# Two zero-padded copies of the rotary key: 128-row score products for the B heads

## The chip, the core and the metric

The kernel runs on one core of one Trainium2 chip. The metric is the device time of one execution in microseconds (us). The core has TensorE (PE, matrix products, with a queue of weight loads shown as PEld), VectorE (DVE), ScalarE (ACT), GpSimd (POOL) and SyncE (SP, which here only starts DMA transfers). Matrix products read SBUF and write PSUM.

## The reference

One residual block of a streaming encoder for 256 tokens of width 2048: a gated feed-forward layer, a mixer with two attention branches A and B, a cross attention to 256 memory tokens, and a second feed-forward layer, each followed by a layer norm. The change touches branch B, cut here to what matters:

```python
q = (c_q @ w_q_b).reshape(b, s, B_HEADS, QK_NOPE + QK_ROPE)        # 16 heads, 128 + 64
q_nope, q_pe = jnp.split(q, [QK_NOPE], axis=-1)
q = jnp.concatenate([q_nope, apply_rope(q_pe, cos, sin)], axis=-1)
k_pe = apply_rope(k_pe[:, :, None, :], cos, sin)                   # one rotary key for all heads
k = jnp.concatenate([k_nope, jnp.broadcast_to(k_pe, ...)], axis=-1)
sc = jnp.einsum('bqhd,bkhd->bhqk', qb, k) * scale                  # masked by chunks, softmax, times v
```

Every head's score is a product over 128 features without position plus one over 64 rotary features. The rotary key is the same for all 16 heads.

## The kernel before, in words

Activations are kept turned, features on the 128 partitions and tokens along the row, so that they can be operands of PE. Weights come in units of 1 MB by SP's queue, and each unit is split by ACT ("hi", a cast to a rounded format) and DVE ("lo", the remainder, L245) so that PE can multiply it in two or three passes with near-fp32 accuracy. Two such units are held at a time. A list of work items (`add`, L143; `run`, L168) is issued in order, and a scheduler then orders each engine's instructions by priorities.

The stages around the change, all in `mixer` (from L783):

- `lat_scale` and `lat_turn` (L850, L868) normalise the low-rank inputs of B and transpose them on PE (L876); ACT (L880) and DVE (L881) empty the PSUM tiles.
- `kpe` (L892) computes the rotary key. A wide product leaves two halves in a PSUM tile, `total` (L269) adds them (L273 on ACT, L274 on DVE) into a work tile `a`. The weight columns were doubled on the host, so rows 0 to 63 and rows 64 to 127 of `a` hold the same 64 features. `swap` (L887) copies blocks of 32 rows crosswise from `a` to `b` with four transfers on SP's queue (L890). DVE then forms a*cos (L897), b*sin (L898) and their sum (L899) in `krope`, 128 rows by 256 tokens.
- `gb_apply` (L434) is woven into this time: gains and biases come by POOL's queue (L440, L441) and DVE applies them (L444, L445).
- The 8 pairs of A heads follow, then the 16 B heads. The rotary queries `rt` hold two heads per tile: an even head in rows 0 to 63, the odd one in rows 64 to 127.
- Per B head h, in this order: `b_scores(h)`, `b_trans(h-1)`, `b_proj(h+2)`, `b_out(h-1)`. `b_scores` calls `scores` (L916), which issues four fp32 products, each of which becomes two instructions on PE (L921): for the first 128 queries against 128 keys and for the second 128 queries against 256 keys, first the part without position (128 rows), then the rotary part (64 rows, upper or lower half by the head's parity). DVE scales and masks (L1037), and `softmax` runs on DVE and ACT (L761 to L768). `b_trans` transposes the probabilities on PE (L773) and ACT copies them (L779). `b_proj` makes queries and keys of head h+2 (L255 on PE, L1026 on ACT and DVE) and, for every fourth head, the values of four heads (L286, L1011). `b_out` multiplies values and probabilities (L962, L963) and splits the result (L234, L235).
- The output projections follow (L299), and later `mem_norm` (L1141) normalises the memory tokens; its `spread` (L1170) multiplies a matrix of ones by diagonal matrices on PE.

A matrix `ones` of 128x128 is kept for the whole kernel: the first use is a run of 12 products at the start (L474), the last is `spread`. Small per-row values (`sm`) have four buffers per name.

Of the kernel before, what the change touches and what calls it, by code (L numbers as in the profile page):

```python
# [9 lines left out]
F32 = mybir.dt.float32  # L10
F32R = mybir.dt.float32r
I32 = mybir.dt.int32
AF = mybir.ActivationFunctionType
ALU = mybir.AluOpType
# [3 lines left out]
P = 128  # L18
S = 256
# [72 lines left out]
class Kernel:  # L92
# [34 lines left out]
    def w1(self, shape=(P, S), dt=F32):  # L127
        return self.work.tile(list(shape), dt, tag="w1", bufs=6, name=self.name("w1"))

    def sm(self, tag, n, dt=F32):  # L130
        return self.small.tile([P, n], dt, tag=tag, name=self.name(tag))

    def mm_tile(self):
        return self.ps_mm.tile([P, 512], F32, tag="mm", name=self.name("mm"))
# [243 lines left out]

    def ln_scale(self, st):
        nc = self.nc  # L380
        mv, v, y, a = self.sm("mv", 2), self.sm("v", 1), self.sm("y", 1), self.sm("a", 1)
        nc.vector.bn_aggr(mv, st)
        nc.vector.tensor_scalar(v, mv[:, 1:2], LN_EPS, None, ALU.add)
        self.rsqrt(v, y, a)
        nb = self.sm("nb", 1)
        self.chain = nc.vector.scalar_tensor_tensor(nb, mv[:, 0:1], -1.0, y, ALU.mult, ALU.mult)
        return mv[:, 0:1], y, nb

# [58 lines left out]

    def setup(self):
        nc, t = self.nc, self.t
        self.ones = self.const.tile([P, P], F32, name="ones")  # L450
        nc.vector.memset(self.ones, 1.0)
        nc.scalar.activation(self.sm("first", 1), self.ones[:, 0:1], AF.Silu)
        self.vecs = self.const.tile([P, N_VEC], F32, name="vecs")
        self.rope = self.const.tile([P, 2, S], F32, name="rope")
        self.ident = self.const.tile([P, P], F32, name="ident")
        make_identity(nc, self.ident)
        self.mask = self.const.tile([P, 3 * P], F32, name="mask")
        nc.gpsimd.memset(self.mask, 0.0)
        self.mask_out(self.mask)
        self.krope = self.const.tile([P, S], F32, name="krope")  # L460
        self.h = [self.res.tile([P, D], F32, tag=f"h{i}", name=f"h{i}") for i in range(2)]

    def mask_out(self, b):
# [319 lines left out]
    def mixer(self, xT, st, steps):  # L783
        nc, t = self.nc, self.t
        SPANS = ((0, P), (P, 3 * P))
        e = self.__dict__
# [4 lines left out]
        def val(n, tts, g, ps, tags=None, held=0, keep=False, again=False):  # L791
            def fn(w=None):
                if keep:
                    kept[g] = w
                w = kept.pop(g) if again else w
                for tt in tts:
                    if g == 0:
                        ps[tt] = self.mm_tile()
                    self.mm_tok(ps[tt], tt, w, xT(), range(4 * g, 4 * g + 4), g == 0, g == 3)
                if g == 3:  # L800
                    if "t" not in va:
                        va["t"] = self.block("H4", (P, 2, 1024))
                    for tt in tts:
                        (nc.vector.tensor_copy if tt else nc.scalar.copy)(
                            va["t"][:, tt, n * 512:(n + 1) * 512], ps[tt])
            ap = t["w_va"][n, :, g * 2048:(g + 1) * 2048]
            self.add(fn, *(() if again else ((ap, tags),)), held=held)

        ps = {}
        first = self.collect(lambda: self.skewed(  # L810
            lambda tt, g, **kw: val(0, (tt,), g, ps, **kw), (),
            (None, None, ("H5", "H0", "early"), ("X0", "X1"))))
        a, b, c = steps(1)
# [35 lines left out]

        def lat_scale():  # L850
            self.lat = self.block("H5", (P, 2, 2, 512))
            v, y, a = (self.sm(n, 4) for n in ("lv", "ly", "la"))
            for tt in range(2):
                for k in range(2):
                    l = self.lat[:, tt, k, :]
                    nc.vector.tensor_tensor(l, lqs["add"][tt, k], lps[tt, k], ALU.add)
                    nc.scalar.activation(self.w2(), l, AF.Square, accum_out=v[:, 2 * tt + k:2 * tt + k + 1])
            nc.vector.tensor_scalar(v, v, 1.0 / LORA, RMS_EPS, ALU.mult, ALU.add)
            self.rsqrt(v, y, a)
            for tt in range(2):  # L860
                for k in range(2):
                    l, r = self.lat[:, tt, k, :], y[:, 2 * tt + k:2 * tt + k + 1]
                    if k:
                        nc.vector.tensor_scalar(l, l, r, None, ALU.mult)
                    else:
                        nc.scalar.mul(l, l, r)
# [15 lines left out]

        self.pair_group(0, t["w_lat"][0], 512, KT, xT, SUMS_IN, fx, lps, lqs, None, SUM_HOME + ("H5",))
        self.add(lat_scale, prio=SOON)
        self.add(lambda: self.gb_apply(0, self.h), prio=LATE)

        def swap(dst, src):  # L887

            for b in range(4):
                nc.sync.dma_start(dst[32 * b:32 * b + 32], src[32 * (b ^ 1):32 * (b ^ 1) + 32])  # L890

        def kpe(w):  # L892
            ps = self.at_tile()
            self.mm_wide(ps, w, xT())
            a, b = self.total(ps), self.w1()
            swap(b, a)
            nc.vector.tensor_tensor(self.krope, a, self.rope[:, 0, :], ALU.mult)  # L897
            nc.vector.tensor_tensor(b, b, self.rope[:, 1, :], ALU.mult)  # L898
            nc.vector.tensor_tensor(self.krope, self.krope, b, ALU.add)  # L899
        self.add(kpe, t["w_kpe"][0])  # L900


# [22 lines left out]
        CAUSAL = ((0, 0, P), (P, 1, S))  # L925
# [103 lines left out]

        def b_scores(h, held):  # L1030
            def fn():
                rows = slice(64 * (h % 2), 64 * (h % 2) + 64)
                ps = scores([(bq.pop((h, 0)), bq.pop((h, 1))),
                             (self.rt[rows, h // 2, :], self.krope[rows])], CAUSAL)
                s = self.w2()
                with self.prio(NEAR):
                    nc.vector.scalar_tensor_tensor(s[:, :3 * P], ps[:, :3 * P], float((NOPE + ROPE) ** -0.5),  # L1037
                                                   self.mask, ALU.mult, ALU.add)
                    self.softmax(s, SPANS)
                bsc[h] = s  # L1040
            self.add(fn, held=held)
# [99 lines left out]
    def mem_norm(self):  # L1141

        nc, t = self.nc, self.t
        e = self.mem = {}

        def load():
            e["m"] = [self.block(f"T{1 + tt}", (P, D)) for tt in range(2)]
            e["raw"] = [self.block(g) for g in ("T3", "H4")]
            for j in range(2):
                nc.gpsimd.dma_start(e["m"][j], t["mem"][j])  # L1150
            for j in range(2):
                nc.gpsimd.dma_start(e["raw"][j], t["memT"][:, 8 * j:8 * j + 8, :])

        def stat():

            e["diag"] = self.w2((P, 4, P))
            for tt in range(2):
                st = self.ln_begin()
                for n in range(4):
                    self.ln_piece(st, e["m"][tt], n)  # L1160
                mean, r, _ = self.ln_scale(st)
                for k, v in enumerate((mean, r)):
                    nc.vector.tensor_scalar(e["diag"][:, 2 * k + tt, :], self.ident, v, None, ALU.mult)
            e["mT"] = self.act(["H0", "H1", "H2", "H3"])

        def spread():

            ps = self.at_tile()
            for j in range(4):
                nc.tensor.matmul(ps[:, j * P:(j + 1) * P], self.ones, e["diag"][:, j, :], start=True, stop=True)  # L1170
            e["mr"] = self.w2((P, 2, 1, S))
            nc.scalar.copy(e["mr"].rearrange("p a o s -> p (a o s)"), ps)

        def quarter(q):
            def fn():
                v = e["raw"][q // 2][:, q % 2 * 4:q % 2 * 4 + 4, :]
                for k, op in enumerate((ALU.subtract, ALU.mult)):
                    nc.vector.tensor_tensor(v, v, e["mr"][:, k].to_broadcast([P, 4, S]), op)
                for j in range(4):
                    kt = 4 * q + j  # L1180
                    nc.scalar.activation(v[:, j, :], v[:, j, :], AF.Identity,
                                         bias=self.vec("mem_ln_b", kt), scale=self.vec("mem_ln_g", kt))
                self.split(v, e["mT"].blk(0, 4 * q, 4), e["mT"].blk(1, 4 * q, 4))
            return fn

        return {0: [load], 3: [stat], 5: [spread], 6: [quarter(0)], 8: [quarter(1)], 10: [quarter(2)], 12: [quarter(3)]}
# [272 lines left out]
```

## Time and profile before

| | us |
|---|---|
| median of 3 runs | 2508.15 (2506.3 to 2508.43) |
| span of the profiled execution | 2508.1 |
| PE busy | 2484.0 |
| PE weight loads busy | 2082.5 |
| DVE busy | 2055.5 |
| ACT busy | 1334.4 |
| POOL busy | 28.3 |
| mean granted clock of PE | 0.997 of full |

All times are device times. The profiled execution's own time is its span, from the first instruction to the last. In the profile, a line such as `L921 PE MATMUL at<-krope,T 64*128 64x256` reads: the instruction of line 921 on PE, writing the PSUM tile `at` from `krope` and `T`; 64*128 is the part of the array that the weights take (rows by columns), and 64x256 is the moving operand (rows by columns). Behind it stand counts and durations, and in brackets the idle time of the engine ahead of it with what ended that. The chain of waits follows the work that ended last back from the end of the kernel. Durations of single instructions on PE overlap with their neighbours, so times from start to start tell what they cost.

### The profile page before, as it was taken

What the parts mean: (1) busy time and instruction counts of PE and PEld (TensorE: products, weight loads), DVE (VectorE), ACT (ScalarE), POOL (GpSimd) and SP (SyncE); (2) the same over time, 40 slices, a digit from 0 to 9 for tenths busy, and PEclk for the clock granted to TensorE, in tenths of its full rate; (3) what the DMA queues carried; (4) which work ended last, traced back from release to release, by engine and by line L of the source; (5) the groups of instructions that cost most, each with busy time, mean ns of one, the idle gap of its engine ahead of it and who ended that gap; (6) DMA issues with size and microseconds to landing.
All of it is one profiled execution on the core that took longest, in us unless ns stands there. A gap on an engine that the chain in (4) does not pass through costs nothing.

```text
span 2508.1 us, 30455 instructions
## 1 busy us (share of the span) xinstructions
PE 2484.0 (99%) x11966; PEld 2082.5 (83%) x11966; DVE 2055.5 (82%) x2312; ACT 1334.4 (53%) x1798; POOL 28.3 (1%) x67
## 2 busy tenths in 40 slices
PE   9999999999999999999999999999999999999998
PEld 8888888889888887888888888888888888888886
DVE  6999889899778988676578798557888988898986
ACT  5555555555455555554444564545555555555552
POOL 0000000000000001000000000000000000000000
PEclk9999999999999999999999999999999999999999
DMA  6655555546645556543456547544554555555553
GB/s 254 240 197 204 189 202 203 207 174 220 233 159 202 208 204 223 182 150 113 154 208 231 187 171 253 195 155 149 211 205 171 203 199 201 201 201 201 200 214 141
DMA packets 72512, 490.03 MB, mean 195 GB/s; under 512 B 8368, under 2 KB 8752, under 8 KB 17200
## 3 DMA queue, kind: packets, MB, share of 16 engines
q1 hardware_dynamic: 66384, 467.11, 51.7%
q0 software_dynamic: 4256, 17.83, 2.2%
q10 hardware_dynamic: 1728, 3.15, 0.3%
q8 instruction: 93, 1.52, 0.2%
q14 instruction: 51, 0.42, 0.0%
HBM read 484.77 MB, written 2.10 MB: 194 GB/s over the span
## 4 chain that ended last, share of the span: by engine, by line
PE 94%; DVE 3%; DMA 2%; ACT 0%; issue 0%; SPq 0%; DVEq 0%; POOL 0%; ACTq 0%; POOLq 0%
PE mm L299 25%; PE at L299 24%; PE mm L353 10%; PE at L353 9%; PE mm L286 8%; PE mm L265 7%; PE mm L267 4%; PE mm L255 2%; PE at L921 2%; DVE lo L245 1%; PE at L286 1%; PE at L773 1%; DMA H<-xT 0%; PE at L1275 0%; PE at L962 0%; PE at L404 0%
## 5 line engine op out<-in xcount | busy, mean ns | idle before, releaser
L242 ACT CAST hi<-raw 128x1024 fp32r<-128x1024 f32 (+1 forms) x848 | 801.9, 988 | 603.7 <-PE at L299 178.5
L245 DVE TENSOR_TENSOR lo<-raw,hi 128x2048 fp32r<-128x2048 f32 (+2 forms) x425 | 904.5, 2129 | 239.2 <-ACT hi L242 237.4
L299 PE MATMUL mm<-hi,T 128*128 128x512 f32 (+1 forms) x1280 | 298.5, 383 | 0.8 <-ACT hi L234 0.8
L242 ACT CAST X<-H 128x1024 fp32r<-128x1024 f32 (+1 forms) x162 | 165.0, 1035 | 220.2 <-DVE H L191 88.4
L299 PEld LDWEIGHTS mm<-hi,T 128*128 128x128 f32 x1280 | 238.0, 188 | 45.5 <-ACT hi L234 1.4
L299 PE MATMUL at<-hi,T 128*128 128x512 f32 x1072 | 257.3, 389 | 0.6 <-DVE w L631 0.6
L245 DVE TENSOR_TENSOR X<-H,X 128x2048 fp32r<-128x2048 f32 (+1 forms) x81 | 182.4, 2251 | 67.6 <-ACT X L242 67.6
L299 PEld LDWEIGHTS at<-hi,T 128*128 128x128 f32 x1072 | 201.1, 188 | 42.7 <-DVE w L631 1.0
L299 PE MATMUL mm<-lo,T 128*128 128x512 f32 (+1 forms) x640 | 153.8, 382 | 0.0
L299 PE MATMUL at<-hi,H 128*128 128x512 f32 x608 | 144.9, 390 | 1.0 <-DVE w L631 1.0
L299 PEld LDWEIGHTS mm<-lo,T 128*128 128x128 f32 x640 | 119.1, 188 | 21.8
L299 PEld LDWEIGHTS at<-hi,H 128*128 128x128 f32 x608 | 113.8, 188 | 25.0 <-DVE w L631 1.4
L299 PE MATMUL at<-lo,T 128*128 128x512 f32 x536 | 132.6, 389 | 0.0
L265 PE MATMUL mm<-T,hi 128*128 128x512 f32 x512 | 124.8, 394 | 0.0
L299 PEld LDWEIGHTS at<-lo,T 128*128 128x128 f32 x536 | 100.6, 188 | 20.9
L299 PE MATMUL mm<-hi,H 128*128 128x512 f32 x480 | 116.0, 391 | 0.0
L191 DVE TENSOR_TENSOR H<-H,raw 128x512 f32<-128x512 f32 (+1 forms) x162 | 109.6, 677 | 1.7
L265 PEld LDWEIGHTS mm<-T,hi 128*128 128x128 f32 x512 | 94.5, 189 | 19.3 <-issue 0.9
L299 PEld LDWEIGHTS mm<-hi,H 128*128 128x128 f32 x480 | 89.2, 188 | 18.5 <-issue 0.3
L189 DVE TENSOR_TENSOR H<-raw 128x1024 f32<-128x1024 f32 (+1 forms) x81 | 97.2, 1199 | 3.8 <-DMA raw<-ffn_w_in 3.0
L353 PE MATMUL mm<-X,X 128*128 128x512 f32 x348 | 95.8, 392 | 1.3 <-DVE H L235 1.3
L242 ACT CAST X<-raw 128x1024 fp32r<-128x1024 f32 (+1 forms) x54 | 55.3, 1036 | 52.6 <-DVE raw L191 31.4
(319 smaller groups left out, 3916.1 us busy)
## 6 DMA issues: line engine op xcount, KB each, us to landing
raw<-ffn_w_in SPq DMA_DIRECT2D x150, 1024.0 KB, 4.6
raw<-ffn_w_out SPq DMA_DIRECT2D x66, 1024.0 KB, 4.6
raw<-w_gate SPq DMA_DIRECT2D x32, 1024.0 KB, 4.7
raw<-ffn_w_out_r SPq DMA_DIRECT2D x16, 1024.0 KB, 4.8
raw<-w_qk SPq DMA_DIRECT2D x16, 1024.0 KB, 4.8
raw<-w_o_b SPq DMA_DIRECT2D x16, 1024.0 KB, 4.7
raw<-w_out SPq DMA_DIRECT2D x16, 1024.0 KB, 4.7
raw<-w_xk SPq DMA_DIRECT2D x16, 1024.0 KB, 4.8
```

The source lines that it names most:

```text
L189: self.nc.vector.tensor_tensor(two[0], two[1], raw[:, :m].unsqueeze(1).to_broadcast([P, 2, m]), ALU.add)
L191: self.nc.vector.tensor_tensor(t[:, a * m:a * m + m], t[:, b * m:b * m + m], raw[:, a * m:a * m + m], ALU.add)
L242: self.nc.scalar.copy(hi[:, c:d], src[:, c:d])
L245: self.nc.vector.tensor_tensor(lo[:, :n], src, hi[:, :n].bitcast(F32), ALU.subtract)
L255: self.nc.tensor.matmul(ps, w[wi][:, cols[j]:cols[j] + P], x.at(xi, kt), start=(j + wi + xi == 0), stop=(j == n - 1 and wi == 1),)
L265: self.nc.tensor.matmul(ps, hi[kt], x.both(kt), start=(kt == 0), stop=False)
L267: self.last_mm = self.nc.tensor.matmul(ps[:, :S], lo[kt], x.at(0, kt), start=False, stop=(kt == n - 1))
L286: self.last_mm = self.nc.tensor.matmul(ps, x.at(xi, kt)[:, tt * P:(tt + 1) * P], w[wi][:, j * 512:(j + 1) * 512], start=(start and j + wi ...
L299: self.last_mm = self.nc.tensor.matmul(ps[tt, g][:, :n], x.at(xi, kt)[:, tt * P:(tt + 1) * P], w[wi][:, c:c + n], start=first and j + wi + ...
L353: self.last_mm = self.nc.tensor.matmul(bank[:, :m], a[xi], v[wi][:, c * m:(c + 1) * m], start=own and first and wi + xi == 0, stop=own and ...
L773: self.nc.tensor.transpose(ps[:, i * P:(i + 1) * P], s[:, c:c + P], self.ident)
L921: nc.tensor.matmul(ps[:, c0:c0 + nk], q[:, tt * P:(tt + 1) * P], k[:, :nk], start=(j == 0), stop=(j == len(parts) - 1))
```

## The change: what it does

`krope` gets two copies side by side, [128, 2, 256], cleared to zero once at the start by POOL. Copy 0 has the rotary key in rows 0 to 63 and zeros below, copy 1 has zeros in rows 0 to 63 and the key in rows 64 to 127. A score's rotary product takes the whole query tile of two heads (128 rows) and copy h % 2, so that the other head's queries meet zeros. In `kpe`, a*cos is written over `a`, and the sum is written by two additions of 64 rows, one for each copy.

To have room, the matrix `ones` is taken from a rotation of six work tiles (`w1`) at the start and made anew by POOL in `mem_norm`, and the small tiles have two buffers or one in place of four.

```diff
-    def sm(self, tag, n, dt=F32):
-        return self.small.tile([P, n], dt, tag=tag, name=self.name(tag))
+    def sm(self, tag, n, dt=F32, bufs=None):
+        return self.small.tile([P, n], dt, tag=tag, name=self.name(tag), **({"bufs": bufs} if bufs else {}))
...
-        mv, v, y, a = self.sm("mv", 2), self.sm("v", 1), self.sm("y", 1), self.sm("a", 1)
+        mv, v, y, a = (self.sm(k, n, bufs=2) for k, n in (("mv", 2), ("v", 1), ("y", 1), ("a", 1)))
...
-        nb = self.sm("nb", 1)
+        nb = self.sm("nb", 1, bufs=2)
...
-        self.ones = self.const.tile([P, P], F32, name="ones")
+        self.ones = self.w1((P, P))
         nc.vector.memset(self.ones, 1.0)
...
-        self.krope = self.const.tile([P, S], F32, name="krope")
+        self.krope = self.const.tile([P, 2, S], F32, name="krope")
+        nc.gpsimd.memset(self.krope, 0.0)
...
-            v, y, a = (self.sm(n, 4) for n in ("lv", "ly", "la"))
+            v, y, a = (self.sm(n, 4, bufs=1) for n in ("lv", "ly", "la"))
...
             swap(b, a)
-            nc.vector.tensor_tensor(self.krope, a, self.rope[:, 0, :], ALU.mult)
+            nc.vector.tensor_tensor(a, a, self.rope[:, 0, :], ALU.mult)
             nc.vector.tensor_tensor(b, b, self.rope[:, 1, :], ALU.mult)
-            nc.vector.tensor_tensor(self.krope, self.krope, b, ALU.add)
+            for j in range(2):
+                rows = slice(64 * j, 64 * j + 64)
+                nc.vector.tensor_tensor(self.krope[rows, j, :], a[rows], b[rows], ALU.add)
...
-                rows = slice(64 * (h % 2), 64 * (h % 2) + 64)
                 ps = scores([(bq.pop((h, 0)), bq.pop((h, 1))),
-                             (self.rt[rows, h // 2, :], self.krope[rows])], CAUSAL)
+                             (self.rt[:, h // 2, :], self.krope[:, h % 2, :])], CAUSAL)
...
+            e["ones"] = self.w1((P, P))
+            nc.gpsimd.memset(e["ones"], 1.0)
...
-                nc.tensor.matmul(ps[:, j * P:(j + 1) * P], self.ones, e["diag"][:, j, :], start=True, stop=True)
+                nc.tensor.matmul(ps[:, j * P:(j + 1) * P], e["ones"], e["diag"][:, j, :], start=True, stop=True)
```

More of the change, by code (lines that the diff above doesn't have):

```diff
@@ L449, in setup @@
         nc, t = self.nc, self.t
-        self.ones = self.const.tile([P, P], F32, name="ones")
+        self.ones = self.w1((P, P))
         nc.vector.memset(self.ones, 1.0)
-        nc.scalar.activation(self.sm("first", 1), self.ones[:, 0:1], AF.Silu)
+        nc.scalar.activation(self.sm("first", 1, bufs=1), self.ones[:, 0:1], AF.Silu)
         self.vecs = self.const.tile([P, N_VEC], F32, name="vecs")
```

## The prediction

> **What bounds the kernel now.** I read the busy shares first, then the shares of the chain of work that ended last.
>
> ```profile
> PE 2484.0 (99%) x11966; PEld 2082.5 (83%) x11966; DVE 2055.5 (82%) x2312; ACT 1334.4 (53%) x1798; POOL 28.3 (1%) x67
> PE 94%; DVE 3%; DMA 2%; ACT 0%; issue 0%; SPq 0%; DVEq 0%; POOL 0%; ACTq 0%; POOLq 0%
> ```
>
> TensorE (PE) is busy for 99% of the span and carries 94% of the chain. Work taken off PE shortens the kernel, as long as nothing else comes late in its place. Next I read the stretch in which the 16 B heads run, from the first to past the last of their score products, as one window (PE, PEld, DVE, ACT, POOL busy us, granted clock, DMA share, GB/s).
>
> ```profile
> 1099.86:1203.84 103.98, 103.98 (x633) 85.43 (x632) 64.32 (x147) 50.55 (x126) 0.00 (x0) 1.00 0.34 120
> ```
>
> PE is covered for all of it at a granted clock of 1.00, VectorE (DVE) for 62%, ScalarE (ACT) for 49%, the DMA engines for 34%. So PE sets the pace here. But "busy" hides how much of it is waiting inside the array. For that I took the chain of waits in order of time in the same stretch (start, us, piece), where each piece lasts until the next one starts:
>
> ```profile
> 1099.86 1.89 PE at L921 x8
> ...
> 1120.04 0.43 PE at L962 x2
> 1120.47 0.22 PE at L963 x2
> 1120.70 1.89 PE at L921 x8
> 1122.59 0.48 PE at L773 x3
> 1123.07 2.87 PE mm L255 x24
> ...
> 1132.48 1.89 PE at L921 x8
> 1134.38 0.43 PE mm L255 x2
> ...
> 1199.00 2.29 PE mm L299 x10
> ...
> 1201.95 1.89 PE at L921 x8
> 1203.84 1.37 PE mm L299 x5
> 1205.21 0.33 PE at L773 x3
> ```
>
> There are 16 pieces "L921 x8 1.89", one per B head, all equal. Each holds eight instructions, two for each fp32 product: no-position part and rotary part for 128 keys, then both for 256 keys. L962 and L963 (values times probabilities) have the same two shapes with full 128x128 weights: 0.43 us for the two instructions of a 256-column product, 0.22 us for those of a 128-column one. At that rate the eight instructions of L921 take 2 x 0.43 + 2 x 0.22 = 1.30 us. They take 0.59 us more. The timeline shows where:
>
> ```profile
> 1120.53 0.39 PE L921 MATMUL at<-w,w 128*128 128x128 f32 x2
> 1120.85 0.49 PE L921 MATMUL at<-krope,T 64*128 64x128 f32 x2
> 1121.26 0.70 PE L921 MATMUL at<-w,w 128*128 128x256 f32 x2
> 1121.89 0.70 PE L921 MATMUL at<-krope,T 64*128 64x256 f32 x2
> 1122.52 0.55 PE L773 MATMUL at<-ident,w 128*128 128x128 f32 x3
> ```
>
> From start to start: 0.32 and 0.41 us where 0.22 would do, 0.63 and 0.63 where 0.43 would do. The products alternate between 128 rows (128*128) and 64 rows (64*128), and every change of form costs 0.1 to 0.2 us. L963 to the first L921 product is 128 rows to 128 rows, and L963 takes its plain 0.22 us. So it is neither the change of operands nor that of the PSUM tile. A last change comes after the piece: three transposes of L773 take 0.48 us behind L921 and 0.33 us elsewhere (the last row of the chain).
>
> **The change part by part.** The rotary products become 128*128 with as many columns as before, so no change of form is left inside a head or behind it. PE's order of instructions in the B heads, as the scheduler gives it, is the same in both kernels.
>
> *Inside L921:* 16 x (1.89 - 1.30) = 9.44 us.
>
> *Behind L921:* in the whole chain of the stretch, 10 of the 16 pieces are followed by L773 x3 at 0.48: 10 x (0.48 - 0.33) = 1.5 us. The other six are followed by products of L255 or L299. Two L255 take 0.43, where 24 take 2.87 (0.12 each): 0.19 us too long. Five L299 take 1.37, where ten take 2.29 (0.23 each): 0.22 too long. At 0.195 for each of six that is 1.17 us. Together 12.1 us off PE.
>
> *What is late next.* Each head's softmax runs on DVE and ACT, and its transposes stand on PE behind the scores of the next head. The tightest place is the head before a group of value products (L286). Here are its DVE rows, and the transposes that wait for them:
>
> ```profile
> 1127.56 2.29 DVE L245 TENSOR_TENSOR lo<-raw,hi 128x2048 fp32r<-128x2048 f32 x1 [1.16 <-ACT hi L242]
> 1129.77 0.55 DVE L1037 SCALAR_TENSOR_TENSOR w<-at,mask 128x384 f32<-128x384 f32 x1
> 1131.87 0.42 DVE L1026 COPY w<-mm 128x256 f32<-128x256 f32 x1 [0.69 <-PE mm L255]
> 1133.62 0.55 DVE L768 TENSOR_SCALAR w<-w,sm_r 128x128 f32<-128x128 f32 x2
> 1134.65 0.27 PE L773 MATMUL at<-ident,w 128*128 128x128 f32 x1
> ```
>
> L768 ends at about 1134.1, 0.5 us before its transposes. The conversion at 1127.56 waits for ACT, not for PE, so it does not move when PE gets faster; L1037 behind it stays at 1129.77. The one wait for PE in that chain is 0.69 us (L1026), and that is all that the softmax can gain: it ends at 1133.4. PE gets there earlier by two heads, 0.74 for the first and 0.59 + 0.19 for the second, about 1.5: at 1133.1. So PE waits about 0.4 us in that head. It occurs three times, and DVE, once behind, starts the next round 0.1 later, so I take 0.4 + 0.5 + 0.6 = 1.5 us. Bounds: none (if the conversion comes earlier after all), and 7.2 us (below). The stretch gives 12.1 - 1.5 = 10.6 us.
>
> *The rotary key itself (kpe).* Before, a*cos was written to krope while four transfers moved a's halves into b. Now it is written over a, so it must stand until those transfers have read a; in the new order it stands right ahead of b*sin, which waits for them anyway.
>
> ```profile
> 959.01 3.31 SPq L890 DMA_DIRECT2D w<-w  x4
> 961.25 0.42 DVE L897 TENSOR_TENSOR krope<-w,rope 128x256 f32<-128x256 f32 x1
> 963.00 0.69 DVE L444 TENSOR_TENSOR h<-h,w 128x512 f32<-128x512 f32 x1
> 968.03 0.42 DVE L898 TENSOR_TENSOR w<-w,rope 128x256 f32<-128x256 f32 x1 [3.54 <-DMA w<-w]
> 968.37 2.29 DVE L245 TENSOR_TENSOR lo<-raw,hi 128x2048 fp32r<-128x2048 f32 x1
> 971.24 0.69 DVE L445 TENSOR_TENSOR h<-h,w 128x512 f32<-128x512 f32 x1
> 971.84 1.29 DVE L444 TENSOR_TENSOR h<-h,w 128x512 f32<-128x512 f32 x2
> 975.58 2.25 DVE L881 SCALAR_TENSOR_TENSOR X<-at,vecs,X 128x256 fp32r<-128x256 f32 x5
> 976.11 0.69 PE L876 MATMUL at<-ident,H 128*128 128x128 f32 x2 [5.68 <-DVE X L881]
> ```
>
> DVE stands 3.54 us until 968.03, and everything behind it waits too; PE then idles 5.68 us until the first L881 frees a PSUM tile. So what stands on DVE between 968.03 and L881 counts in full. Before: 7.55 us. After, in the scheduler's new order: a*cos and b*sin 0.34 each (968.03 to 968.37), one sum of L274 and two 64-row additions at about 0.33 each, conversion 2.21 (968.37 to 970.58, where the krope addition starts), one L445 0.60, conversion 2.2, L274 0.33: 7.0 us. One L445 and two L444 less than before, of which one L444 slipped into the wait. L881 starts about 0.5 us earlier. The 64-row additions are not in the trace; they have 256 columns like the 0.42 us of L897, so 0.3 each is the likely value, bounds 0.15 and 0.42 each. If the new order's two conversions wait for something, the gain is gone: bounds -0.8 and +1 us. I take -0.5.
>
> *The rest, at nothing.* Clearing krope adds a memset on POOL at the start and the second "ones" one before the memory norm. Their nearest rows:
>
> ```profile
> 0.89 0.42 POOL L458 MEMSET mask<- 128x384 f32 x1
> 1301.68 0.55 POOL L1150 DMA_DIRECT2D T<-mem  x1 [239.19 <-DMA raw<-w_o_b]
> L1170 PE MATMUL at<-w,ones x8: 272/275/275, 1363.9 to 1364.7; 128*128 128x128 f32 x8
> ```
>
> The first, some 0.6 us, stands ahead of no early consumer: krope is next written at 961. The second stands in POOL's queue ahead of the loads of mem; POOL sat idle 239 us before these, and the tile that it clears is one of six in a rotation whose last users are the B heads, done by 1204. If that cover were gone, a late memset would hold back loads of which the first consumer is some 60 us away: under 0.5 us. Buffers of the small tiles go from four to two or one; the next user of each comes one layer norm later, so no wait is added. SP's queue, with the same transfers in the same order, is passed by nothing.
>
> The sum: 2508.1 - 10.6 - 0.5 = **2497.0 us**. The profiled execution's span of 2508.1 is 0.05 below the median of the runs, 2508.15, so I carry it over as it is.
>
> **The rivals.**
>
> *Softmax paces the heads.* If DVE comes late not only in three heads but in the 13 others too, at 0.44 us each, the waits are 1.5 + 5.7 = 7.2 us and the time 2508.1 - 12.1 + 7.2 - 0.5 = 2502.7. For it: L1037 starts behind a conversion, not right behind the scores, in the head shown. Against: DVE has 38% of the stretch free, and after each group of value products it catches up.
>
> *The change doesn't do what it says:* the extra time belongs to the rotary operands or to the accumulation into a PSUM tile, not to the form. Then only kpe's 0.5 us remains: 2507.6. Against it: 0.48 for L773 behind L921, though L773 touches neither.
>
> *Slower: full-row weight loads are no longer covered.* Rows of the groups by form:
>
> ```profile
> L921 PEld LDWEIGHTS at<-w,w 128*128 128x128 f32 x64 | 9.6, 190 | 1.9
> L921 PEld LDWEIGHTS at<-krope,T 64*128 64x128 f32 x64 | 9.4, 184 | 7.2 <-issue 5.3
> ```
>
> If a load of all 128 rows had to wait for the product before it, as none of other rows would be free, all 128 loads of L921 would stand in the open: 128 x 0.19 = 24.3 us against the 12.1 saved, so 2508.1 + 24.3 - 12.1 - 0.5 = 2519.8. It decides from 64 uncovered loads on. Against it: L962 does two full-row loads and two products in 0.43 us, where 0.19 more for each would give 0.81. [...]
>
> *Slower: the swap transfers.* Two multiplications, not one, now stand behind them. They would have to land after 979 instead of 968 to eat 11.1 us; each us later is one us of PE's idle time before L876. Nothing on SP's queue changed, so I give it little.
>
> *More than forecast:* no wait for the softmax, and L881 a few us earlier: 2494.5 or less.
>
> **How the numbers follow.** Forecast, 2494.5 to 2499.5: 0.74. Softmax paces: 0.12. No effect: 0.05. Uncovered loads: 0.03. Late transfers: 0.02. More: 0.04. The range 2493 to 2503 holds the forecast, nearly all of the softmax rival and half of "more", some 0.87; the bounds of the waits (0 to 7.2) and of kpe (-0.8 to +1) lie in it. Faster by over 0.2% (about what a measurement of this kernel can tell from no change; under 2503.1) is 0.89, within 0.06, slower 0.05.
>
> **What would show it.** Right: L921 x8 at 1.30 instead of 1.89 in each of 16 pieces, L773 behind it at 0.33, rows "128*128" for krope, the stretch of the heads shorter by some 10 us, everything from 1204 on shifted by as much. A wait "L773 <- DVE L768" of about 0.4 us three times shows the softmax; more of them is the first rival. L921 still near 1.89 shows the second; PE's loads without overlap the third. PE's idle time before L876 should be near 5.2. The forecast is wrong if PE's order is kept but the time between starts is not 0.11 and 0.21.

## The result, and the profile after

| | before | changed kernel |
|---|---|---|
| median of 5 runs, us | 2507.94 (2506.3 to 2508.43) | 2494.74 (2491.78 to 2496.15) |
| ratio to before, 95% interval | | 0.9947 (0.9936 to 0.9957) |
| span of the profiled execution, us | 2508.1 | 2491.9 |

The change makes the kernel 13.2 us faster. In two later comparisons, each on one chip against its own runs of the kernel before, it was 12.6 us (2494.89 against 2507.49, ratio 0.9948, 0.9935 to 0.9962) and 11.1 us (2495.40 against 2506.46, ratio 0.9957, 0.9944 to 0.9971). The forecast was 11.1 us, to 2497.0.

The busy shares and the chain's shares of the changed kernel, as the page has them:

```profile
PE 2471.8 (99%) x11966; PEld 2082.8 (84%) x11966; DVE 2055.1 (82%) x2313; ACT 1332.9 (53%) x1798; POOL 28.8 (1%) x69
PE 95%; DVE 2%; DMA 1%; ACT 1%; issue 0%; SPq 0%; DVEq 0%; ACTq 0%; POOL 0%
```

PE loses 12.2 us of busy time with the same 11966 products, DVE and ACT hardly any, and PE still carries nearly the whole chain. The waiting had counted as "busy". The window over the B heads (from the first score piece's start to the start of what follows the last, columns as before):

```profile
1097.24:1190.30 93.06, 92.94 (x633) 85.92 (x633) 63.40 (x146) 50.12 (x126) 0.21 (x1) 1.00 0.37 128
```

103.98 us have become 93.06, 10.92 less, at the same granted clock of 1.00. Now the chain of waits there (start, us, piece), with the rows that answer to those of before:

```profile
1115.13 0.43 PE at L965 x2
1115.56 0.22 PE at L966 x2
1115.78 1.31 PE at L924 x8
1117.09 0.33 PE at L774 x3
1117.42 2.87 PE mm L255 x24
...
1126.11 1.31 PE at L924 x8
1127.43 0.23 PE mm L255 x2
...
1188.99 1.31 PE at L924 x8
1190.30 1.17 PE mm L299 x5
```

(Lines are shifted by one to three: L921 is L924 now, L962 is L965, L773 is L774.) All 16 score pieces take 1.31 us instead of 1.89, the transposes behind them 0.33 instead of 0.48, two products of L255 0.23 instead of 0.43, five of L299 1.17 instead of 1.37. The four starts inside a head:

```profile
1115.62 0.39 PE L924 MATMUL at<-w,w 128*128 128x128 f32 x2
1115.84 0.39 PE L924 MATMUL at<-krope,T 128*128 128x128 f32 x2
1116.07 0.60 PE L924 MATMUL at<-w,w 128*128 128x256 f32 x2
1116.50 0.59 PE L924 MATMUL at<-krope,T 128*128 128x256 f32 x2
1116.93 0.49 PE L774 MATMUL at<-ident,w 128*128 128x128 f32 x3
```

From start to start 0.22, 0.23, 0.43 and 0.43 us, where it was 0.32, 0.41, 0.63 and 0.63. The columns are the same; only the rows of the rotary weights went from 64 to 128.

**Where the whole difference lies.** PE runs the same products in nearly the same order in both kernels, so the n-th product's start in one trace can be taken from that in the other. The difference grows in these places (us, profiled execution against profiled execution; elsewhere it moves by 0.4 us at most):

```
                                     changed   again   third   rows of 64 only (e2)
first layer norm, at 690                0.7     0.9     0.3     -0.3
rotary key and lat_turn, 969 to 983     1.9     0.5     1.8      1.6
the 16 B heads                         11.0    11.0    11.0      0.0
from 1838 to the end                    2.8     1.2     2.6      2.5
```

The B heads repeat to 0.1 us. In the second line, "again" has only 0.5 because its clock was halved there for 6.83 us and not for 3.41 (last section), which costs 1.7 us of PE's work. In the stages of the first and the last line the change touches only the buffers of the small tiles, and these are not the cause: e1, which has none of the change's edits, shows 0.4 and 2.5 us there. The last line stands, with 1.2 to 3.9 us, in all other profiles but that of e6, in which PE waits 1.9 us for DVE at one place there (L353): the profiled execution of before lost time there that others don't. Nor does a span hold all of an execution: in the changed kernel's profiled run the span is 2491.9 and the device time 2493.65, 1.75 us more, and in every run that has both on record the difference is 1.72 to 1.85 us, also in all 44 of the kernel before.

### The profile page after: what moved, and what is told of

The parts are those of the page before. It is cut to its first block, busy times and chain, and to the rows that moved or that the text cites. A ratio compares the mean times of both kernels' runs of the same rounds, so it can differ in the third digit from the quotient of the medians.

```text
span 2491.9 us, 30464 instructions
## 1 busy us (share of the span) xinstructions
PE 2471.8 (99%) x11966; PEld 2082.8 (84%) x11966; DVE 2055.1 (82%) x2313; ACT 1332.9 (53%) x1798; POOL 28.8 (1%) x69
## 4 chain that ended last, share of the span: by engine, by line
PE 95%; DVE 2%; DMA 1%; ACT 1%; issue 0%; SPq 0%; DVEq 0%; ACTq 0%; POOL 0%
PE mm L299 25%; PE at L299 25%; PE mm L353 10%; PE at L353 10%; PE mm L286 8%; PE mm L265 7%; PE mm L267 4%; PE mm L255 2%; PE at L924 1%; PE at L286 1%; DVE lo L245 1%; PE at L774 1%; DMA H<-xT 0%; PE at L1279 0%; PE at L404 0%; PE at L1255 0%
## 5 line engine op out<-in xcount | busy, mean ns | idle before, releaser
L242 ACT CAST hi<-raw 128x1024 fp32r<-128x1024 f32 (+1 forms) x848 | 801.8, 987 | 604.2 <-PE at L299 182.6
L245 DVE TENSOR_TENSOR lo<-raw,hi 128x2048 fp32r<-128x2048 f32 (+2 forms) x425 | 904.3, 2129 | 239.6 <-ACT hi L242 237.8
L299 PE MATMUL mm<-hi,T 128*128 128x512 f32 (+1 forms) x1280 | 298.4, 383 | 1.4 <-ACT hi L234 1.4
L242 ACT CAST X<-H 128x1024 fp32r<-128x1024 f32 (+1 forms) x162 | 164.9, 1034 | 216.7 <-DVE H L191 86.6
L299 PEld LDWEIGHTS mm<-hi,T 128*128 128x128 f32 x1280 | 238.0, 188 | 46.1 <-ACT hi L234 2.0
L299 PE MATMUL at<-hi,T 128*128 128x512 f32 x1072 | 257.0, 389 | 0.0
L245 DVE TENSOR_TENSOR X<-H,X 128x2048 fp32r<-128x2048 f32 (+1 forms) x81 | 182.3, 2251 | 67.7 <-ACT X L242 67.7
L299 PEld LDWEIGHTS at<-hi,T 128*128 128x128 f32 x1072 | 201.2, 188 | 41.9
L299 PE MATMUL mm<-lo,T 128*128 128x512 f32 (+1 forms) x640 | 153.8, 382 | 0.0
L299 PE MATMUL at<-hi,H 128*128 128x512 f32 x608 | 144.7, 390 | 0.9 <-DVE w L632 0.9
L299 PEld LDWEIGHTS mm<-lo,T 128*128 128x128 f32 x640 | 119.1, 188 | 21.8
L299 PEld LDWEIGHTS at<-hi,H 128*128 128x128 f32 x608 | 113.9, 188 | 24.7 <-DVE w L632 1.3
L299 PE MATMUL at<-lo,T 128*128 128x512 f32 x536 | 132.6, 389 | 0.0
L299 PEld LDWEIGHTS at<-lo,T 128*128 128x128 f32 x536 | 100.6, 188 | 20.9
L299 PE MATMUL mm<-hi,H 128*128 128x512 f32 x480 | 116.1, 392 | 0.0
L299 PEld LDWEIGHTS mm<-hi,H 128*128 128x128 f32 x480 | 89.3, 188 | 18.2 <-DVE w L274 0.2
L353 PE MATMUL mm<-X,X 128*128 128x512 f32 x348 | 95.9, 392 | 0.0
L242 ACT CAST X<-raw 128x1024 fp32r<-128x1024 f32 (+1 forms) x54 | 55.4, 1035 | 51.5 <-DVE raw L191 31.9
```

Source lines behind the costliest of these rows:

```text
L242: self.nc.scalar.copy(hi[:, c:d], src[:, c:d])
L245: self.nc.vector.tensor_tensor(lo[:, :n], src, hi[:, :n].bitcast(F32), ALU.subtract)
L299: self.last_mm = self.nc.tensor.matmul(ps[tt, g][:, :n], x.at(xi, kt)[:, tt * P:(tt + 1) * P], w[wi][:, c:c + n], start=first and j + wi + ...
L353: self.last_mm = self.nc.tensor.matmul(bank[:, :m], a[xi], v[wi][:, c * m:(c + 1) * m], start=own and first and wi + xi == 0, stop=own and ...
```

## The experiments

The theory: PE pays about 0.19 us each time its products change between 128 and 64 rows, and the padded key takes all of these changes out of the B heads; what is given back is a wait for the softmax; around the rotary key the DVE's order gains a little. The rivals are named with each run.

### Two changes of form instead of four (e1)

The kernel before, with the loops of `scores` exchanged; nothing is padded.

```diff
-            for c0, tt, nk in spans_q:
-                for j, (q, k) in enumerate(parts):
+            for j, (q, k) in enumerate(parts):
+                for c0, tt, nk in spans_q:
                     nc.tensor.matmul(ps[:, c0:c0 + nk], ...,
-                                     start=(j == 0), stop=(j == len(parts) - 1))
+                                     start=(j == 0 and c0 == 0), stop=(j == len(parts) - 1 and c0 > 0))
```

> The kernel before, with the four score products of a B head in another order: both products without position (128 rows) first, then both rotary products (64 rows); 64-row products and the single rotary key stay. Theory (every change between 128-row and 64-row form costs some 0.19 us, in both directions): two changes per head in place of four, so the pieces L921 x8 fall from 1.89 to about 1.50 (0.22 + 0.43 + 0.41 + 0.43), the transposes behind them stay at 0.48, and the kernel gains 16 x 0.38 = 6 us: about 2502. Rival (each weight load of 64 rows stands in the open, wherever it stands): pieces at 1.69, a gain of 3.2 us: 2504.7. Rival (the operands or the PSUM accumulation cost the time): pieces at 1.89, 2507.9.

Measured: 2500.36 us against 2507.49, ratio 0.9972 (0.9962 to 0.9983). Chain of waits of this kernel:

```profile
1118.16 1.51 PE at L921 x8
1119.66 0.48 PE at L773 x3
1120.14 2.87 PE mm L255 x24
```

The pieces take 1.51, as the theory said, not 1.69 or 1.89, and the transposes keep their 0.48. The stretch of the heads is 6.2 us shorter. So the price belongs to the change of form, in either direction (0.21 us from 128 to 64 rows inside the piece, 0.15 back to 128 behind it), and not to each 64-row load nor to the operands: the same products with the same operands cost 0.38 us less per head when they are sorted. The piece is the plain 1.30 and one change, so the 64-row products in themselves take as long as full-row ones.

### Everything but the 128-row products (e2)

```diff
+                rows = slice(64 * (h % 2), 64 * (h % 2) + 64)
...
-                             (self.rt[:, h // 2, :], self.krope[:, h % 2, :])], CAUSAL)
+                             (self.rt[rows, h // 2, :], self.krope[rows, h % 2, :])], CAUSAL)
```

> The changed kernel with one thing undone: the rotary score products read 64 rows again (of copy h % 2), all other edits stay. Theory (the 128-row form is what gains): pieces L924 x8 back at 1.89, transposes behind them at 0.48, the stretch of the B heads as long as before (104 us); what remains is the gain around the rotary key, 0.5 to 2 us: 2506 to 2507.5. Rival (the other edits carry the gain): near 2494.7.

Measured: 2506.55 against 2507.49, ratio 0.9996 (0.9987 to 1.0005). Chain of waits:

```profile
1119.51 1.89 PE at L924 x8
1121.40 0.48 PE at L774 x3
1121.88 2.87 PE mm L255 x24
```

The pieces are back at 1.89 and the heads' stretch is as long as before, to 0.02 us. The side edits (two copies, `ones` twice, small buffers, the new order around the rotary key) are worth 0.9 us in the medians, which this measurement can't tell from nothing.

### Where the softmax holds PE up (e6)

The changed kernel with three lines of `softmax` left out:

```diff
-        nc.vector.reciprocal(r, r)
-        for i, (a, b) in enumerate(spans):
-            nc.vector.tensor_scalar(s[:, a:b], s[:, a:b], r[:, i:i + 1], None, ALU.mult)
```

> The changed kernel without the normalisation of all softmaxes (reciprocal and the two multiplications by it are left out, so probabilities are not divided by their sums). Theory (PE waits about 0.3 us for the softmax in three of the B heads): the chain of a head is shorter by 0.7 us, these waits vanish, and the stretch of the B heads is 0.8 to 1.0 us shorter than in the changed kernel, pieces L924 x8 still at 1.31. Rival (PE is not held up there by the softmax): the stretch is the same to 0.1 us.

In the changed kernel the weight loads' waits in and right behind the heads' stretch, then the chain of waits and the timeline at the second of the three places, read:

```profile
PEld at L774 <- DVE w L769: 0.9, 3, 0.4
PEld at L774 <- PE at L924: 0.2, 1, 0.2
```

```profile
1146.26 2.00 ACT hi L242 x2
...
1148.29 2.29 DVE lo L245
1150.58 0.47 DVE w L1039
...
1153.62 0.30 DVE w L769
...
1153.96 0.33 PE at L774
```

```profile
1153.44 0.47 PE L255 MATMUL mm<-X,hi 128*128 128x256 f32 x1
1153.62 0.55 DVE L769 TENSOR_SCALAR w<-w,sm_r 128x128 f32<-128x128 f32 x2
1153.96 0.33 PE L774 MATMUL at<-ident,w 128*128 128x128 f32 x1
```

The chain leaves PE here: the conversion (L242, L245) comes late, the softmax behind it (L1039 to L769) too, and the transposes of L774 wait for it. From the start of the last product of L924 (1153.20) to the L255 that is the fourth behind it (1154.62) 1.42 us pass, where the instructions between take 1.12 at their plain rate (0.43 for L924, three L255 at 0.12, three L774 at 0.11): PE loses 0.3. Counted so, it loses 0.2, 0.3 and 0.3 us at the three places. The rows above divide this otherwise: of the 0.9 us, 0.35 each belongs to the second and the third place and 0.2 to the transposes right behind the last head (0.46 us for three, where 0.33 would do), and at the first place the trace names L924 and not the softmax. Without the normalisation the stretch from the start of the first score product to that of the last is 92.41 us against 92.85, although the scheduler now puts four more products of L255 (0.48 us) and one less of L299 (0.23) into it: like for like 0.7 us shorter. Its first score piece takes 1.51 us instead of 1.31, since it now stands right behind products of 128x64 weights (L963, 128*64, another change of form); without that it would be 0.9. No wait ahead of the transposes is left in the stretch. The theory holds, with its 0.8 to 1.0. The one time of this run, 2498.44, says nothing here: in its lat_turn PE idled 4.6 us, and all softmaxes have changed.

### The rotary key: order, wait and landing (e3, and the changed kernel again)

e3 gives a*cos a tile of its own, so that it waits for no transfer:

```diff
-            nc.vector.tensor_tensor(a, a, self.rope[:, 0, :], ALU.mult)
+            c = self.w1()
+            nc.vector.tensor_tensor(c, a, self.rope[:, 0, :], ALU.mult)
...
-                nc.vector.tensor_tensor(self.krope[rows, j, :], a[rows], b[rows], ALU.add)
+                nc.vector.tensor_tensor(self.krope[rows, j, :], c[rows], b[rows], ALU.add)
```

> The changed kernel with a*cos of the rotary key written to a tile of its own, so that it waits for no transfer. Theory (PE's idle time ahead of the lat_turn transposes is set by when the swap transfers land and by the DVE work between that and the first L882 or its like): behind the landing stand 0.34 + 2.21 + 0.67 + 0.33 + 0.60 + 0.60 + 2.2 + 0.33 = 7.3 us instead of 7.2, so nothing is lost or won by 0.3 us beside the scatter of the landing: 2494 to 2496, idle time 3.7 to 5.5 us. Rival (the write over a, by its wait, made the gain there): idle time at 5.7 as before, about 2 us slower than the changed kernel: 2496.6. B heads as in the changed kernel.

> The changed kernel once more. Theory: the B heads' stretch repeats to 0.1 us (about 93.1 us from the first to the end of the last score piece, 10.9 less than before), while PE's idle time ahead of the lat_turn transposes scatters with the landing of the swap transfers, 3.5 to 5.5 us; the time is 2494.7 within 2 us. Rival (the gain around the rotary key belongs to the change): idle time again at 3.6 within 0.2.

> The changed kernel once more, beside e7 and e8 on the same chip. Theory: B heads' stretch 10.9 us under before; idle time ahead of lat_turn's second half 3.5 to 5 us with a half-clock window of 3.4 or 6.8 us behind it; 2494 to 2496.

Measured: 2495.09 (e3), 2494.89 and 2495.40 (the changed kernel twice); e3's ratio is 0.9954 (0.9941 to 0.9966). First the changed kernel's DVE rows, then what PE waited for in the second of its profiles and in that of e3:

```profile
957.78 2.49 SPq L891 DMA_DIRECT2D w<-w  x4
965.23 0.43 DVE L898 TENSOR_TENSOR w<-w,rope 128x256 f32<-128x256 f32 x1 [1.71 <-DMA w<-w]
966.24 0.85 DVE L902 TENSOR_TENSOR krope<-w,w 64x256 f32<-64x256 f32 x2
972.46 2.91 DVE L882 SCALAR_TENSOR_TENSOR X<-at,vecs,X 128x256 fp32r<-128x256 f32 x7
972.99 0.44 PE L877 MATMUL at<-ident,H 128*128 128x128 f32 x2 [3.58 <-DVE X L882]
```

```profile
PE at L877 <- DVE X L882: 4.1, 1, 4.1
```

```profile
PE at L877 <- DVE X L882: 4.0, 1, 4.0
```

From the first multiplication after the landing to the first evacuation (the first L882, which empties a PSUM tile for PE) DVE needs 7.23 us, in all three profiles of the changed kernel and in e2; before, 7.55, also in e1, which has the old order. That part is the change's, 0.3 us. The rest is when the multiplication can start: 7.45 us after the first swap transfer's issue here, 7.1 in the third profile, 6.9 in e3, against 9.0 in the kernel before and 8.2 in e1. In the second profile DVE came to it 5.7 us after that issue and found the data there. PE's idle time is 5.7 and 4.8 us in the old order, 3.6, 4.1, 3.9, 3.9 (e2), 4.2 (e5) and 4.6 (e6) in the new. So the write over `a` is not what gains (e3 has it not and idles 4.0), and the rival falls. Whether the transfers land earlier because of the change or by chance, two profiles of the old order do not settle; but e4 and e9 below, with the same four transfers, land the last one 7.9 and 8.0 us behind the first issue, like e1 (8.0), so nothing here shows that the change brings them forward.

### Taking the rotary key and the gains out of lat_turn's way (e4, e7, e9)

These go beyond the change: can the idle time before L877 be had as well? e4 makes the multiplications and additions an item of low priority behind the first pair of A heads; e7 also raises lat_turn's priority. The edits, cut:

```diff
+            kr.extend((a, b))                      # e4: kpe ends here,
+        def kpe_rope():                            # its DVE work becomes an item
...
+                self.add(kpe_rope, prio=LATE)      # e4: behind a_scores(0)
...
-        self.add(lat_turn)
+        self.add(lat_turn, prio=SOON)              # e7
```

> The changed kernel with the two multiplications and two additions of the rotary key taken out of kpe's item and made an item of their own, of low priority, behind the first pair of A heads, so that DVE meets no wait for the swap transfers ahead of lat_turn. Theory (PE's idle time ahead of the second half of the lat_turn transposes is the DVE work and wait ahead of its first evacuation): DVE goes on at about 963.5 instead of 965.2, with 7.5 us of work ahead of the evacuation instead of 7.2, so the idle time falls from 3.6 to 4.1 to about 2; the half-clock window behind it (3.4 us at 0.5) may go with it. Gain on the changed kernel 1.5 to 3.5 us: 2491 to 2493.5. Rival (something else sets that idle time): 2494.8, idle time unchanged. B heads as in the changed kernel, 10.9 us under before.

> The kernel with the late rotary key (e4) and lat_turn at a higher priority, so that its evacuations on DVE come ahead of gains and conversions. Theory: the first evacuation comes one conversion behind 963.5, at about 966.5, earlier than PE runs out of other work at 969.4; the idle time of 3.6 to 4.1 us vanishes and with it the half-clock window after it, up to 1.7 us more: 4 to 5.5 us less than the changed kernel, 2489.3 to 2491. Rival (the conversion that is put off comes late for PE, or the half clock comes anyway): 2491 to 2494. B heads unchanged.

> The kernel of e7 once more, for comparison on the same chip. Theory: no half-clock window behind lat_turn, B heads' stretch 10.9 us under before, 2490.5 to 2492.5.

Measured: e4 2493.42, ratio 0.9947 (0.9934 to 0.9961); e7 2491.43, 0.9939 (0.9927 to 0.9952); e7 again 2493.99, 0.9951 (0.9938 to 0.9963), 1.4 us under the changed kernel on the same chip. What PE waits for at lat_turn in e4, then in e7:

```profile
PE at L877 <- DVE X L882: 2.3, 1, 2.3
```

```profile
PE at L877 <- ACT H L867: 2.1, 1, 2.1
```

In e4 the idle time fell as forecast, and the half clock stayed (3.41 us). In e7 it did not vanish but moved: PE now waits ahead of the first L877, for the normalised inputs (L867), 2.1 us, and 2.3 in the repeat. The forecast for e7 missed that, and its time missed the range; so did the repeat's, where the half clock came back for 3.41 us. The cause stands in e8's timeline, where the same wait is longest: DVE meets the first gain of `gb_apply`, still in transfer, in the middle of the normalisation.

```profile
958.28 0.69 DVE L444 TENSOR_TENSOR h<-h,w 128x512 f32<-128x512 f32 x1 [4.40 <-DMA w<-gb]
958.89 0.15 DVE L370 SCALAR_TENSOR_TENSOR ly<-la,ly 128x4 f32<-128x4 f32 x1
...
965.23 1.97 PE L877 MATMUL at<-ident,H 128*128 128x128 f32 x8 [4.10 <-ACT H L867]
```

e9 takes e8 (below) and moves `gb_apply(0)` behind the first pair of A heads.

> The kernel of e8 (late rotary key, earlier lat_turn, rotary products in pairs) with gb_apply moved behind the first pair of A heads, so that its first L444, which stood 2.6 to 4.4 us for a transfer in the middle of the normalisation of the low-rank inputs, stands there no more. Theory (in e7 and e8 PE's idle time of 2.1 to 4.1 us ahead of the first L877 comes from that wait): PE's idle time at lat_turn falls under 1 us, no half-clock window follows, the region gains 6 to 8 us on the kernel before and the B heads 12.2: 2488 to 2490. Rival (gains now stand among the softmaxes of the A heads and make PE wait there): 2491 to 2493, with waits of PE at L774 or L924 and their like between 985 and 1030.

Measured: 2489.07, ratio 0.9924 (0.9911 to 0.9938). Its window over lat_turn:

```profile
960.00:985.00 25.00, 25.00 (x152) 21.81 (x151) 18.51 (x30) 14.12 (x29) 0.71 (x1) 1.00 0.61 215
```

PE is covered for all 25 us at full clock. By product number the region is 6.8 us shorter than in the kernel before; 1.8 us are given back soon after, mostly where PE waits 1.6 us for a conversion (L245). The forecast holds, and with the first L444 moved the wait ahead of L877 is gone, so the cause named above is the right one.

### Two heads' rotary products side by side (e5, e8)

```diff
+                if h % 2 == 0:                       # both heads' 64-row products first
+                    pre.update({h: self.at_tile(), h + 1: self.at_tile()})
+                    for c0, tt, nk in CAUSAL:
+                        for j in range(2):
+                            rows = slice(64 * j, 64 * j + 64)
+                            nc.tensor.matmul(pre[h + j][:, c0:c0 + nk], self.rt[rows, h // 2, tt * P:(tt + 1) * P],
+                                             self.krope[rows, j, :nk], start=(c0 == 0), stop=False)
...                                                  # then each head's products without position:
+                for c0, tt, nk in CAUSAL:
+                    nc.tensor.matmul(ps[:, c0:c0 + nk], ..., start=False, stop=(c0 > 0))
```

> The changed kernel with 64-row rotary products again, but those of two heads issued side by side, one in the upper and one in the lower half of the array, ahead of both heads' products without position (which then accumulate onto them). Theory (a change of form costs 0.19 us per direction, and two 64-row products in different halves run at the same time, as the A heads' do: eight instructions in 0.86 us): a pair of heads takes 0.86 + 0.38 + 2 x 0.65 = 2.54 us of PE against 2.62 padded, or 2.35 if one of the changes is within the 0.86; so 0.6 to 2.2 us less than the changed kernel over eight pairs: 2492.7 to 2494.3. Rival (the halves do not overlap): 1.30 + 0.38 + 1.30 = 2.98 per pair, 2.9 us more: 2497.7. The softmax waits may move by half a us.

Measured: 2494.84, ratio 0.9953 (0.994 to 0.9965). Chain of waits at the first pair:

```profile
1098.66 0.86 PE at L1042 x8
1099.52 0.85 PE at L1046 x4
1100.37 1.91 PE mm L255 x16
1102.29 0.66 PE at L1046 x4
```

Eight 64-row instructions of two heads take 0.86 us, where in sequence they would take 1.30: the halves do work at the same time. Four steps side by side come to 0.65 at the plain rate, so the change into the 64-row form lies within the 0.86; the first full-row products behind them take 0.85 instead of 0.66, the change back. A pair takes 2.37 us against 2.62 padded, and by product number the heads' stretch is 12.2 us under before instead of 11.0. Eight pairs should have given 2.0 us more and gave 1.2; PE now idles 0.3 us for the softmax (L774 for L769) at three places, 0.8 in all, which fits. The whole time shows nothing of it, and the forecast of 2492.7 to 2494.3 was missed; in this run's profile PE idled 4.2 us at lat_turn and ran at half clock for 6.8 us afterwards.

> Both improvements in one kernel: the late rotary key with the earlier lat_turn (e7), and the rotary products of two heads side by side in the two halves of the array (e5). Theory (the two places are far apart and do not touch): the B heads' stretch 12.2 us under before as in e5, the stretch around lat_turn 4.6 us under before as in e7, together about 1.2 us less than e7: 2490.2. Rival (they share DVE, so that one gives back the other's gain): 2491.4 or more.

Measured: 2492.22, ratio 0.9942 (0.9929 to 0.9954), on the chip of e7's repeat (2493.99) and the changed kernel (2495.40). The heads gain 12.2 us as in e5. The forecast of 2490.2 was missed: lat_turn shows the 4.1 us wait above, with 6.83 us of half clock behind it, and that region gains 0.3 us on the kernel before, not 4.6. The rival's number came out, but not for its reason: the heads kept their gain. With that wait gone, e9 is the fastest version here, 18.5 us under the kernel before.

## Why the prediction was right

**The bound.** Right: what PE lost in the heads came off the end. At 1206 the difference of the starts was 13.6 us, and no more than 0.2 of it was lost behind.

**Inside L921 and behind it (12.1 us).** Right, in each term: 1.31 for 1.30, 0.33 for 0.33, 0.23 and 1.17 for 0.24 and 1.15. e1 separates the cause (change of form) from 64-row loads and operands; e2 shows that nothing else of the change carries it. A change costs 0.19 us on the mean here (12.1 us over 64 changes); what goes on in the array during that time, no run here shows. e1 halves the changes and gets half of it (6.2 us).

**The softmax (1.5 us given back).** The mechanism was right, at the three places, with the conversion ahead of it that waits for ACT; the size was too large: by PE's starts 0.8 us, by e6 0.9. The waits are 0.2, 0.3 and 0.3 us. The first was put at 0.4, though the working itself gives 0.3 (1133.4 less 1133.1), and that DVE falls further behind from round to round (0.4, 0.5, 0.6) does not show: the third wait is no longer than the second.

**The rotary key (0.5 us).** The DVE work fell from 7.55 to 7.23, where I had 7.0: I put the sums at 0.33 each, and the two 64-row additions took 0.85 together (0.42 each, my upper bound; L898 took 0.43 for 128 rows, so half the rows cost as much as all here), and the work behind them starts 0.88 us after the first of them. Yet PE's idle time fell by 2.1 us in the profile compared, to 3.6 where 5.2 was forecast, and by 1.1 to 2.1 over all profiles of the new order against it, because the transfers landed earlier. That they land where they did was taken for granted; they do not, from one execution to the next. That the whole time still came out within the range, and better than forecast, owes something to this luck.

**The sum.** 11.1 forecast, 13.2, 12.6 and 11.1 measured; the interval of the first comparison reaches from 10.8 to 16.1, so it does not tell 13.2 from the forecast. In the terms, the heads gave 11.0 where 10.6 was forecast, the rotary key 0.5 to 1.9 where 0.5 was, and the rest is scatter between executions. One step compared unlike things: "I carry it over as it is" sets the span of the profiled execution beside the median of device times. With the 1.72 to 1.85 us that lie outside the span in every run on record, that execution took some 2509.9 us, about 1.9 more than the median; its own time is not on record. That the two numbers agreed to 0.05 was chance. It did not harm the sum, whose 2508.1 fits the median, but it is why the two traces differ by 16.2 us and the medians by 13.2: the profiled execution of before was 1.9 us over its median, that of the changed kernel 1.1 under.

**The rivals.** Softmax pacing all heads: it does in three, and a little behind the last. Operands, not form: e1 excludes it. Uncovered full-row loads: excluded by 1.31. The loads' rows:

```profile
L924 PEld LDWEIGHTS at<-krope,T 128*128 128x128 f32 x64 | 10.9, 191 | 0.8
L924 PEld LDWEIGHTS at<-w,w 128*128 128x128 f32 x64 | 9.7, 192 | 0.0
```

The idle time ahead of krope's loads went from 7.2 to 0.8 us, of 10.9 us that the 64 loads are busy: here full-row loads are hidden behind full-row products. That a full-row load has to wait for the product before it was this rival's assumption; in these rows it does not. Late transfers: they came earlier.

## What to carry to other kernels

A lone product over 64 rows saved no time here (e1: a piece with two of them took 1.51 us, the plain 1.30 and one change), and among products over 128 rows it cost a change of form on each side, 0.19 us each on the mean, hidden in PE's "busy". Read it from starts, not from durations: compare the same columns in one form and in mixed forms. Three cures, in rising order of work: sort the products by form (6 us here), pad with zeros (11 us), or place two 64-row products in the two halves at once (12 us).

## What the runs showed of the hardware that I had not expected

In every profile but those of e7 and e9, PE's granted clock was halved for some us behind its idle time at lat_turn. Window rows of the kernel before and of the changed kernel behind their idle times (granted clock is the third column from the end):

```profile
976.00:985.00 9.00, 8.89 (x46) 7.65 (x47) 7.70 (x14) 4.06 (x7) 0.00 (x0) 0.83 0.38 123
```

```profile
973.00:982.00 9.00, 9.00 (x45) 7.99 (x46) 7.24 (x13) 4.22 (x7) 0.00 (x0) 0.81 0.37 139
```

A mean of 0.81 over 9 us is 3.4 us at half clock (9 x 0.19 x 2). In the records of the clock it is 3.41 us in the kernel before and in the changed kernel, 6.83 us in its repeat, in e5 and in e8, and none in e7 and e9; it came after idle times of 2.3 us (e4, e7's repeat) as well as 5.7 us, and stayed away after one of 2.1 (e7).

The records also show what goes with it in these runs. Before, the stretches between two changes of the clock are 969.385 us full, 3.413 half and 1518.931 full, which is 284, 1 and 445 times 3.413 us; in the changed kernel 969.385, 3.413 and 1505.278, which is 284, 1 and 441 times. So within these executions the clock changed on a grid of 3.413 us, and what tells the cases apart is how long PE was busy within one cell of it. In the last cell ahead of a half clock, PE was busy for 0 of 3.41 us (before), 1.33 (changed kernel), 1.12 (e4) and 1.15 (e7's repeat). After cells with 1.68 us (before, one cell earlier), 1.92 (changed kernel, one cell earlier) and 1.98 and 2.70 (e7) the clock stayed full; no profile here contradicts this. So the 2.3 us of e4, all in one cell, cost 3.41 us of half clock, and the 2.1 us of e7, split over two cells, cost none. At half clock, 1.90 us (the repeat) and 2.06 (e8) of a cell did not bring the full clock back, 2.9 (before) did.

Half clock for 3.41 us costs 1.7 us of PE's work, for 6.83 us 3.4. So idle times of 2.1 to 4.2 us at lat_turn came here with a further 0 to 3.4 us, which fits that single microseconds there did not add up in the whole times of e5 and e7.
